# One pending weight subtraction, placed ahead of the closing steps of the output projection

## The chip, the cores and the metric

The kernel runs on one core of one Trainium2 chip. The metric is the device time of one execution in microseconds (us); less is better. The core has a matrix engine (PE, whose weight loads PEld overlap the products), a vector engine (DVE), a scalar engine (ACT), a second elementwise engine (POOL), and a queue engine (SP) that issues nearly all DMAs. Each engine works through its own instructions in program order and waits on semaphores for the others.

## The reference

One decoder layer over x of 512 tokens by 2048 channels, all in float32:

```
h = rms_norm(x);  proj = h @ w_in          # 30 column tiles of 128
out_a, out_b, out_c = dilated attention, convolution module, sliding-window attention
x = x + concat(out_a, out_b, out_c) @ w_out          # output projection, residual
h2 = rms_norm(x)
x = x + (silu(h2 @ w_gate) * (h2 @ w_up)) @ w_down   # D_FF = 5632
```

The change lies between the third line and the first product with w_gate.

## The kernel before, in words

Tokens lie along the free axis (512 columns), channels along the 128 partitions. Weights come from HBM as units of 128 x 1024 float32. To keep float32 precision each unit is split into two fp32r parts: a high part `wh` (a cast on ACT) and a low part `wl = w - wh` (a subtraction on DVE, line 221). Products are then summed from high and low parts.

The units are numbered in the order of their use: 0 to 60 for the input projection, 61 to 92 for the output projection (two passes over the 16 column tiles, one unit for each tile and pass), and from 93 on for the feed-forward part. There the matrices gate, up and down are multiplied in seven products of half size in place of eight (a Strassen form). Each group takes four weight blocks called 11, 12, 21 and 22, and sums of them called s; its seven products use the units s, 11, 21, s, 12, 22, s in this order, with the operands number 5, 1, 7, 6, 2, 4, 3 of the activations. The first group is g0, the first of gate: units 93 (s), 94 (11), 95 (21), 96 (s), 97 (12), 98 (22), 99 (s).

`next_unit()` hands out unit u and emits the split of unit u+2 (`split_up_to`), so a split runs two units ahead. The low part's subtraction is first put into the list `lows`. While the list `late_lows` is filled (from the input projection to the end of the output projection), it stays there until the next call of `lows_now()`, which comes with the next unit; afterwards it is emitted at once. In the second pass of the output projection, from its third tile on, and in all that follows, ACT casts each unit twice (lines 240 and 241): into a PSUM tile `wn`, from which DVE subtracts, and into the SBUF tile `wh`. There are three `wh`, three `wl` and two PSUM buffers.

`Ticks` is an order written out by hand: a step is entered as due so many ticks later, `tick()` emits what is due, and `drain()` emits all that is left. In the second pass a tile has two ticks. The steps on a finished tile n of x2 = x + mix @ w_out are: `residual` (line 825: the PSUM sum into x), a tick later `scale_x2` (the store to DRAM, and the product with the norm's gain on ACT), then `differences` (lines 855 or 861 to 863 on DVE: the operand sums of the Strassen form) and `square_x2` (for the norm), then `high` (ACT, line 869) and `low` (DVE, line 875), which make the operands `h5_j`, `h1_j` and so on for the feed-forward products. The tiles come in the order 0, 8, 1, 9, ..., 7, 15.

After the last tile (n = 15, unit 92) `ticks.drain()` emits what is left: the low parts of the operands of pair 6, the differences of tile 7, `residual` of tile 15, and all that follows from these two tiles. Then line 912 calls `lows_now()`, which emits the subtraction of unit 94, the one still pending, and, where a raw weight buffer is free, further loads (`pump`). Only then does the first group begin: `next_unit()` for unit 93, with the sum s + 11 on DVE (line 176) and the split of unit 95 ahead of it.

A product of the feed-forward part is `Block.multiply`: eight matmuls with the high weights over 512 columns (the operand's high and low half side by side), and eight with the low weights over 256 columns. `flip` alternates the order: unit 93 takes the high weights first and then the low ones, unit 94 the low ones first, unit 95 the high ones first, and so on.

The norm's factor is worked out within the first group: `norm2a` after unit 95 (eight small matmuls, line 303, one DVE step on line 369, a power on POOL, line 370), `norm2b` after unit 96 (four transposes, line 309).

Of the kernel before, what the change touches and what calls it, by code (L numbers as in the profile page):

```python
# [109 lines left out]
def kernel(ctx: ExitStack, tc: tile.TileContext, xT, wi, wo, wgu, wd, cst_in, outT):  # L110
# [8 lines left out]
    def open_banks(**pools):  # L119
        if psum:  # L120
            psum.pop("stack").close()
        psum["stack"] = ctx.enter_context(ExitStack())
        for name, bufs in pools.items():
            psum[name] = psum["stack"].enter_context(
                tc.tile_pool(name=f"{name}{len(pools)}", bufs=bufs, space=bass.MemoryType.PSUM))
# [7 lines left out]
    def bank(name, cols=T):  # L133
        return psum["banks"].tile([P, cols], F32, name=name, tag="b")
# [71 lines left out]
    def pump(limit):  # L206
        while at["entry"] < len(entries) and len(raws) < limit and entries[at["entry"]][0] not in held:
            buf, key, parts = entries[at["entry"]]
            t, o = take(buf, key, sum(p.shape[-1] for p in parts)), 0
            for part in parts:  # L210
                nc.sync.dma_start(t[:, o:o + part.shape[-1]], part)
                o += part.shape[-1]
            at["entry"] += 1
# [4 lines left out]
    def lows_now():  # L218
        while lows:
            fn, *args = lows.pop(0)  # L220
            fn(*args)  # L221
        if late_lows:
            pump(RAW_EARLY if at["use"] <= 20 else RAW_BUFS)
# [28 lines left out]
    def next_unit():  # L252
        sums_now()
        u = at["use"]
        at["use"] += 1
        lows_now()
        split_up_to(u + SPLIT_AHEAD)
        if not lows:
            pump(RAW_EARLY if u < 20 else RAW_BUFS)
        return splits.pop(u)  # L260

    def mm3(out, wh, wl, xh, xl, start, stop):
        nc.tensor.matmul(out, wh, xh, start=start, stop=False)  # L263
        nc.tensor.matmul(out, wh, xl, start=False, stop=False)  # L264
        nc.tensor.matmul(out, wl, xh, start=False, stop=stop)  # L265
# [540 lines left out]
    def load_x(i):  # L806
        if i < KT:
            n = OUT_ORDER[0][i]
            xr[n] = slot(f"xr{n}")
            nc.sync.dma_start(xr[n], xT[n])  # L810
# [66 lines left out]
    def split_rows(k):  # L877
        for name in ROWS[k:k + 3]:
            if name in mix:
                split_mix(name)  # L880
# [4 lines left out]
    for half in range(2):  # L885
        for i, n in enumerate(OUT_ORDER[half]):
            if half == 1 and i == 2:
                ticks.drain()
                b = None
                open_banks(banks=4, high=2)  # L890
            b = bank(f"o{half}_{n}")
            wh, wl = next_unit()
            for kk in range(8):
                k = 8 * half + kk
                row = ROWS[k]
                while row not in m_hi and row not in mix:
                    ticks.tick()
                split_rows(k)
                s = slice(kk * P, (kk + 1) * P)
                mm3(b, wh[:, s], wl[:, s], m_hi[row], m_lo[row], kk == 0, kk == 7)  # L900
                if kk % 4 == 3 or i == 0:
                    ticks.tick()
            ticks.after(0, residual, n, b, half)
            if half == 0:
                load_x(i + 2)
        for row in ROWS[8 * half:8 * half + 8]:
            if half == 0:
                m_hi.pop(row), m_lo.pop(row)
    ticks.drain()
    m_hi = m_lo = r1b = mult_a = bias_a = bias_c = None  # L910

# [323 lines left out]
```

## Time and profile before

| | |
|---|---|
| median of 3 runs | 1929.77 us (1929.02 to 1929.9) |
| the profiled execution, time | 1930.23 us |
| the profiled execution, span of its instructions | 1928.4 us |
| mean granted clock of PE | 0.995 |
| DVE busy | 1470.9 us (76%) |
| ACT busy | 1328.8 us (69%) |
| POOL busy | 985.3 us (51%) |

The span runs from the first to the last instruction of the profiled execution; the time of an execution holds a little besides. A row of the timeline reads: start, length, engine, line of the kernel, operation, output and inputs, shapes, the number of merged instructions, and in brackets how long the engine sat idle before it and what released it. An instruction's length includes what overlaps with the next one, so the distance from start to start is often shorter than the length. A row of the view by stretches gives the stretch, its length, the busy time of each engine with the number of instructions, the granted clock of PE (PEclk, 1.00 is full speed), the busy share of the DMA engines and the GB/s.

### The profile page before, as it was taken

How to read it: one execution, taken by the hardware profiler on the slowest of the kernel's cores; microseconds unless marked ns; L12 is line 12 of the kernel's file. 1: busy time of each engine (PE TensorE's matmuls, PEld its weight loads, DVE VectorE, ACT ScalarE, POOL GpSimd, SP SyncE). 2: the span in 40 equal slices, each digit the busy share in tenths (PEclk: the TensorE clock that was granted, in tenths of full speed). 3: DMA queues.
4: the chain of work that ended last, by engine and by line, in shares of the span. 5: the costliest groups of instructions: out<-in, count | busy, mean ns of one | idle time of the engine just before them, and what ended most of it. 6: DMA issues, size and time to landing. Idle time of an engine off the chain costs nothing.

```text
span 1928.4 us, 29205 instructions
## 1 busy us (share of the span) xinstructions
PE 1897.9 (98%) x10332; PEld 1644.2 (85%) x10332; DVE 1470.9 (76%) x2512; ACT 1328.8 (69%) x1782; POOL 985.3 (51%) x636
## 2 busy tenths in 40 slices
PE   8999999989999999999999999999999999999999
PEld 7888788878887888888888888888888788888888
DVE  6799989997578677777777777777777577767776
ACT  6356555553356788788888888888887577667675
POOL 0111011000000788778887878788776656656564
PEclk9999999999999999999999999999999899999999
DMA  7232222223342344444444444353438978777685
GB/s 264 76 102 70 66 88 77 72 77 115 131 135 73 129 160 162 139 160 167 160 142 156 162 158 155 138 179 139 173 126 302 363 274 278 267 247 272 198 281 194
DMA packets 125651, 319.48 MB, mean 166 GB/s; under 512 B 14016, under 2 KB 29504, under 8 KB 125504
## 3 DMA queue, kind: packets, MB, share of 16 engines
q1 hardware_dynamic: 125360, 317.51, 47.8%
q8 instruction: 81, 1.33, 0.3%
q14 instruction: 66, 0.54, 0.1%
q10 hardware_dynamic: 144, 0.10, 0.0%
HBM read 259.09 MB, written 57.15 MB: 164 GB/s over the span
## 4 chain that ended last, share of the span: by engine, by line
PE 71%; DMA 1%; DVE 0%; issue 0%; ACT 0%; SPq 0%; DVEq 0%
PE out L966 66%; PE o L264 1%; PE o L263 1%; PE o L265 1%; DMA a<-od 1%; DMA od<-u21st 0%; DVE h L875 0%; DVE xr L825 0%; DVE ssum L90 0%; DVE wl L221 0%; ACT wn L240 0%; ACT wh L241 0%; PE n2b L303 0%; DVE ml_b L753 0%; PE r2s L309 0%
## 5 line engine op out<-in xcount | busy, mean ns | idle before, releaser
L966 PE MATMUL out<-h,wh 128*128 128x512 f32 x2464 | 590.4, 392 | 0.1
L966 PEld LDWEIGHTS out<-h,wh 128*128 128x128 f32 x2464 | 454.8, 189 | 88.0 <-DVE h L875 0.6
L966 PEld LDWEIGHTS out<-h,wl 128*128 128x128 f32 x2464 | 316.9, 192 | 15.7 <-DVE wl L221 3.8
L966 PE MATMUL out<-h,wl 128*128 128x256 f32 x2464 | 321.1, 284 | 3.6 <-DVE wl L221 3.6
L966 PE MATMUL out<-a,wh 128*128 128x512 f32 x1232 | 300.3, 395 | 3.0 <-DMA a<-od 2.0
L966 PEld LDWEIGHTS out<-a,wh 128*128 128x128 f32 x1232 | 227.4, 190 | 49.9 <-DMA a<-od 3.6
L234 ACT CAST wh<-w 128x1024 fp32r<-128x1024 f32 (+1 forms) x93 | 96.8, 1041 | 131.4 <-PE o L264 48.2
L966 PEld LDWEIGHTS out<-a,wl 128*128 128x128 f32 x1232 | 160.9, 193 | 10.6 <-DMA a<-od 4.1
L966 PE MATMUL out<-a,wl 128*128 128x256 f32 x1232 | 164.6, 285 | 2.3 <-DMA a<-od 2.3
L221 DVE TENSOR_TENSOR wl<-w,wh 128x1024 fp32r<-128x1024 f32 (+1 forms) x93 | 112.4, 1209 | 30.1 <-ACT wh L234 29.9
L978 DVE TENSOR_TENSOR y<-y,out 128x256 f32<-128x256 f32 x120 | 50.5, 421 | 65.8 <-PE out L966 62.1
L442 DVE SCALAR_TENSOR_TENSOR y<-bu,cst,y 128x511 f32<-128x511 f32 (+14 forms) x120 | 88.7, 739 | 0.5
L370 POOL TENSOR_TENSOR n2r<-n2v,nhalf 128x4 f32<-128x4 f32 x1 | 1.0, 1010 | 162.3 <-DVE n2v L369 162.3
L264 PE MATMUL o<-ml_c,wh 128*128 128x512 f32 x128 | 50.4, 394 | 3.3 <-DVE ml_c L753 3.3
L979 DVE TENSOR_TENSOR y<-y,out 128x256 f32<-128x256 f32 x120 | 50.5, 421 | 4.1
L263 PE MATMUL cq<-hh,wh 128*128 128x512 f32 x128 | 51.3, 401 | 0.0
L263 PE MATMUL o<-mh_c,wh 128*128 128x512 f32 x128 | 51.0, 399 | 0.0
L265 PE MATMUL o<-mh_c,wl 128*128 128x512 f32 x128 | 50.1, 391 | 0.0
L265 PE MATMUL cq<-hh,wl 128*128 128x512 f32 x128 | 50.1, 391 | 0.0
L264 PE MATMUL cq<-hl,wh 128*128 128x512 f32 x128 | 50.0, 391 | 0.0
L825 DVE TENSOR_TENSOR xr<-xr,o 128x512 f32<-128x512 f32 x32 | 21.9, 685 | 21.7 <-PE o L265 21.7
L264 PEld LDWEIGHTS o<-ml_c,wh 128*128 128x128 f32 x128 | 24.1, 188 | 9.2 <-DVE ml_c L753 4.8
(3092 smaller groups left out, 4817.4 us busy)
## 6 DMA issues: line engine op xcount, KB each, us to landing
a<-od SPq DMA_DIRECT2D x196, 256.0 KB, 5.4
w<-in_wi SPq DMA_DIRECT2D x59, 512.0 KB, 3.6
w<-in_wo SPq DMA_DIRECT2D x32, 512.0 KB, 3.6
y<-x2d SPq DMA_DIRECT2D x48, 256.0 KB, 5.5
x2d<-y SPq DMA_DIRECT2D x64, 128.0 KB, 3.4
x<-in_xT SPq DMA_DIRECT2D x16, 256.0 KB, 7.2
xr<-in_xT SPq DMA_DIRECT2D x16, 256.0 KB, 3.9
x2d<-xr SPq DMA_DIRECT2D x16, 256.0 KB, 2.0
```

What stands on the lines that cost most here:

```text
L221: fn(*args)
L234: nc.scalar.copy(hi[:, :n], t[:, :n])
L263: nc.tensor.matmul(out, wh, xh, start=start, stop=False)
L264: nc.tensor.matmul(out, wh, xl, start=False, stop=False)
L265: nc.tensor.matmul(out, wl, xh, start=False, stop=stop)
L370: nc.gpsimd.tensor_tensor(r, v, nhalf[:, :NT], op=ALU.pow)
L442: nc.vector.scalar_tensor_tensor(yconv[j][:, i:], hconv[j][:, :T - i], c, yconv[j][:, i:], op0=ALU.mult, op1=ALU.add)
L825: nc.vector.tensor_add(t, t, b)
L966: nc.tensor.matmul(out, lhs[:, s], rhs, start=begin, stop=x is xs[-1] and low == flip[0], skip_group_check=True)
L978: sign(out, out if first is None else first, main)
L979: sign(out, out, rest)
```

## The change

One line is added behind the two passes of the output projection:

```diff
@@ -906,6 +906,7 @@
         for row in ROWS[8 * half:8 * half + 8]:
             if half == 0:
                 m_hi.pop(row), m_lo.pop(row)
+    lows_now()
     ticks.drain()
     m_hi = m_lo = r1b = mult_a = bias_a = bias_c = None
 
```

`lows_now()` is:

```python
    def lows_now():
        while lows:
            fn, *args = lows.pop(0)
            fn(*args)
        if late_lows:
            pump(RAW_EARLY if at["use"] <= 20 else RAW_BUFS)
```

So the pending subtraction of unit 94 stands on DVE ahead of everything that `ticks.drain()` emits, and the call on line 912 finds the list empty. No instruction is added or removed.

## The prediction

> **What bounds the kernel now.** I read the page's totals first, then the stretches behind the changed place, then the timeline around it.
>
> ```profile
> span 1928.4 us, 29205 instructions
> PE 1897.9 (98%) x10332; PEld 1644.2 (85%) x10332; DVE 1470.9 (76%) x2512; ACT 1328.8 (69%) x1782; POOL 985.3 (51%) x636
> ```
>
> ```profile
> 640.00:1480.00 840.00, 840.00 (x4830) 742.97 (x4829) 627.53 (x861) 690.71 (x819) 671.77 (x431) 1.00 0.45 158
> 1480.00:1516.00 36.00, 30.72 (x130) 22.50 (x129) 17.81 (x29) 17.12 (x25) 14.85 (x13) 0.86 1.05 391
> 1516.00:1928.40 412.40, 408.64 (x2347) 360.90 (x2345) 296.45 (x458) 284.59 (x316) 247.96 (x158) 1.00 0.75 257
> ```
>
> PE sets the end. From 640 to 1480 us it is busy in 840.00 of 840.00 us, so what arrives earlier at 640 arrives earlier at 1480. From 1480 to 1516 the DMA engines are full (1.05) and PE waits for them; behind that PE is busy again in 408.64 of 412.40 us. A microsecond won on PE near 620 therefore counts, unless the stretch at 1480 swallows it.
>
> The timeline at the changed place, all engines, cut to the rows I use:
>
> ```profile
> 608.23 1.00 ACT L240 CAST wn<-w('11', 'g0')_5530 128x1024 fp32r<-128x1024 f32 x1
> ...
> 613.18 0.42 DVE L875 TENSOR_TENSOR h<-ta,h 128x256 fp32r<-128x256 f32 x1
> ...
> 614.86 0.42 DVE L855 TENSOR_TENSOR ta<-h 128x256 f32<-128x256 f32 x1
> ...
> 615.68 0.40 ACT L869 CAST h<-h 128x256 fp32r<-128x256 f32 x1
> ...
> 616.63 0.69 DVE L825 TENSOR_TENSOR xr<-xr,o 128x512 f32<-128x512 f32 x1 [1.35 <-PE o L265]
> ...
> 617.35 0.72 ACT L835 ACTIVATE h<-xr,cst 128x512 f32<-128x512 f32 x1 [1.26 <-DVE xr L825]
> ...
> 618.30 0.19 PEld L966 LDWEIGHTS out<-h,wh 128*128 128x128 f32 x1 [0.55 <-DVE h L875]
> ...
> 618.64 1.12 PE L966 MATMUL out<-h,wl 128*128 128x256 f32 x8
> ...
> 621.65 1.04 ACT L241 CAST wh<-w('21', 'g0')_5427 128x1024 fp32r<-128x1024 f32 x1
> ...
> 622.04 1.22 DVE L221 TENSOR_TENSOR wl<-w('11', 'g0')_5530,wn 128x1024 fp32r<-128x1024 f32 x1
> 623.17 1.22 DVE L176 TENSOR_TENSOR w('s', 'g0')_5630<-w('s', 'g0')_5630,w('11', 'g0')_5530 128x1024 f32<-128x1024 f32 x1
> ...
> 623.31 2.08 PE L966 MATMUL out<-h,wl 128*128 128x256 f32 x8 [3.55 <-DVE wl L221]
> ```
>
> PE ends unit 93 (the rows at 618.30 and 618.64) and then sits idle for 3.55 us until the low part of unit 94, which is multiplied first, is there (622.04 + 1.22 = 623.26). Its input `wn` was cast long before (608.23 + 1.00 = 609.23): the subtraction waited for nothing but its place in DVE's queue, behind the last steps on x2. The idle time has a second price, which the stretches show in the column PEclk:
>
> ```profile
> 618.96:622.38 3.42, 0.80 (x7) 0.59 (x5) 3.39 (x9) 3.31 (x7) 0.00 (x0) 1.00 0.00 0
> 622.38:625.79 3.41, 2.48 (x10) 2.39 (x11) 3.41 (x4) 1.68 (x3) 0.00 (x0) 0.50 0.00 0
> 625.79:629.20 3.41, 3.41 (x10) 2.64 (x9) 2.50 (x3) 1.91 (x3) 0.00 (x0) 0.50 0.75 234
> ```
>
> After a stretch with PE busy for only 0.80 of 3.42 us the granted clock falls to 0.50, and stays there until 629.20. So the units 94 and 95 run at half speed.
>
> **The change part by part.** Nothing is added or removed: one DVE subtraction moves up.
>
> The new place. What `drain` emits on DVE begins with the row at 613.18 (low parts of pair 6), then the differences of tile 7 (614.86), then `residual` of tile 15 (616.63). The subtraction now stands before 613.18. Its `wn` is ready, and the `wl` buffer that it takes is unit 91's, whose products were over when the last tile began, so it should run at once. It holds DVE for 1.13 us (622.04 to 623.17), and the six operations behind it slip by that. The cover is the 1.35 us for which DVE stood idle before 616.63, since `residual` waits for PE's last product. That leaves 0.2 us. On ACT the casts behind the differences slip from 615.68 to 616.81, ending at 617.2, in front of the scaling at 617.35, which waited 1.26 us; it does not move. So the operand for unit 93's last pair comes as before (618.30). Without that cover unit 93 would end up to 1.13 us later, and no more.
>
> SP's and POOL's queues. The call also runs `pump`, now ahead of x2's last stores. It should issue nothing there: the next load, u0's block 21, needs the raw buffer that g0's 21 holds until unit 95 is split. In the trace it goes out right behind that split's subtraction; it will come with it, about 1.1 us earlier. POOL has nothing to do there.
>
> ```profile
> 624.30 1.22 DVE L221 TENSOR_TENSOR wl<-w('21', 'g0')_5427,wn 128x1024 fp32r<-128x1024 f32 x1
> 624.42 1.02 ACT L240 CAST wn<-w('s', 'g0')_5630 128x1024 fp32r<-128x1024 f32 x1 [1.73 <-DVE w('s', 'g0')_5630 L176]
> ...
> 625.48 1.22 DVE L221 TENSOR_TENSOR wl<-w('s', 'g0')_5630,wn 128x1024 fp32r<-128x1024 f32 x1
> 625.59 0.33 SPq L211 DMA_DIRECT2D w('21', 'u0')_5913<-in_wgu  x1
> ...
> 626.79 1.23 DVE L176 TENSOR_TENSOR w('s', 'g0')_5630<-w('s', 'g0')_5630,w('12', 'g0')_5633 128x1024 f32<-128x1024 f32 x1
> ...
> 628.84 0.69 DVE L973 TENSOR_REDUCE g0u<-out 128x256 f32<-128x512 f32 x1 [0.82 <-PE out L966]
> ...
> 629.45 1.21 DVE L221 TENSOR_TENSOR wl<-w('12', 'g0')_5633,wn 128x1024 fp32r<-128x1024 f32 x1
> ...
> 631.69 0.95 PE L303 MATMUL n2b<-ones,ssum 128*128 128x1 f32 x8
> ...
> 632.50 1.20 PE L966 MATMUL out<-h,wl 128*128 128x256 f32 x8
> ...
> 632.67 0.16 DVE L369 TENSOR_SCALAR n2v<-n2b 128x4 f32<-128x4 f32 x1 [2.02 <-PE n2b L303]
> ...
> 632.92 1.01 POOL L370 TENSOR_TENSOR n2r<-n2v,nhalf 128x4 f32<-128x4 f32 x1 [162.34 <-DVE n2v L369]
> ...
> 633.53 2.00 PE L966 MATMUL out<-h,wh 128*128 128x512 f32 x8
> ...
> 635.38 0.60 PE L309 MATMUL r2s<-ident,n2r 128*128 128x128 f32 x4
> ```
>
> Term 1, the idle time. Eight low matmuls take 8 x 0.12 us at full clock (1.12 us less the 0.28 us length of the last, over 7). Unit 94 starts at 618.64 + 0.96 = 619.60 in place of 623.31: 3.71 us won.
>
> Term 2, the clock. From 623.31 to the norm's matmuls at 631.69 the units 94 and 95 took 8.38 us. At full clock a high matmul costs 0.23 us (2.00 less 0.39 over 7), so two units are 16 x 0.23 + 16 x 0.12 = 5.6 us: 2.78 us won.
>
> Term 3, what is late next. Unit 94 would end at 619.60 + 0.96 + 1.84 = 622.40, but unit 95 begins with its high part, which ACT finishes at 622.69 behind its own x2 steps, unmoved. PE starts 0.05 us behind that (as 623.31 behind 623.26) and loses another 0.1 us on a start after a stall (618.30, next product 618.64): 0.44 us lost. Unit 95's low part comes by 623.17 + 1.22 = 624.39 and is needed at 624.7, so it is hidden, by 0.3 us. The norm's matmuls then start at about 625.65.
>
> Term 4, the norm's factor. DVE now does, one behind the other: the sum s + 11 at 622.04, unit 95's subtraction at 623.17, unit 96's at 624.35 (its cast starts at 623.29 and takes 1.02), the sum with 12 at 625.66 (1.31 behind, as now), the reduction at 626.8, unit 97's subtraction at 627.4, the norm's step at 628.55. POOL follows 0.25 us later and takes 1.01: 629.8. The transposes could start on PE at 625.65 + (635.38 - 631.69) = 629.34, and wait until 629.85: 0.51 us lost. DVE's queue takes the stalled place here, but only for half a microsecond.
>
> Sum: 3.71 + 2.78 - 0.44 - 0.51 = 5.54 us. It is the same as the distance of the transposes, 635.38 to 629.85. From there on all starts about 5.5 us earlier. On the profiled execution (1930.23 us, span 1928.4 and 1.8 us around it) that gives 1924.7; the median of the runs lies 0.46 us below that execution, so I predict 1924.3.
>
> A rule weighed against the row. The row says: 0.80 us busy in 3.42 us was enough for the half clock. The Trainium skill, "TensorE: Matmul & The Clock Gate", Part 1, has the clock halved after an idle window of about 3.4 us, in windows that run free of the kernel. A gap of 3.55 us would hold such a window whole in few executions only; by that rule most runs of before had no half clock, and term 2 would be missing (the first rival below gives that time from rows). This trace does not bear the rule out to the letter, as its window was not idle.
>
> **The rivals.**
>
> First, the clock term is not in the timed runs. Then before starts the norm's matmuls at 623.31 + 5.6 = 628.9 and its transposes at 632.6; against 629.85 the gain is 2.75 us and the time 1927.0. For it: the fall of the clock hangs on where the gap lies. Against it: three runs lie within 0.9 us of each other and within 1.2 us of the profiled one that has the term.
>
> Second, the change doesn't do what it says: the subtraction is held by a buffer until PE's last product of the projection, or the stall goes over to another wait of the same length, such as unit 95's high part. The rows speak against it. ACT's cast is unmoved and done at 622.69, so the longest stall that can follow is the 0.44 us above; and held until 616.6 the subtraction costs unit 93 the 1.13 us that I priced. What is left is a wait that no row shows. It would give about 1929.5.
>
> Third, the other side: the stretch from 1480 to 1516, where the clock falls too.
>
> ```profile
> 1496.19:1499.60 3.41, 2.25 (x9) 1.20 (x8) 0.84 (x2) 0.00 (x0) 0.00 (x0) 1.00 1.05 402
> 1499.60:1503.02 3.42, 2.25 (x6) 1.25 (x4) 0.00 (x0) 0.00 (x0) 1.55 (x1) 0.50 1.04 389
> ...
> 1506.43:1509.84 3.41, 3.41 (x15) 3.17 (x15) 0.00 (x0) 0.53 (x1) 3.33 (x5) 0.50 1.04 405
> ```
>
> Here 2.25 of 3.41 us busy were enough, and the half clock held for 10.2 us. All changes of the clock in these rows lie whole multiples of 3.41 us apart (622.38, 629.20, 1499.60, 1509.84), so work that comes 5.5 us earlier is shifted against them by 1.6 such windows, and the clock may fall earlier here, or stay down into the stretch in which PE is full again. A window of full work at half clock costs 1.71 us. From the fourth further window on (6.8 us) it eats the whole gain; with five the time is 1924.3 + 8.5 = 1932.8. Against it: a window with PE busy throughout ended it both times, and while PE waits for DMA a slow clock costs little. It may as well shorten; I allow 1.7 us, one window, either way inside the forecast.
>
> **How the numbers follow.** The forecast (gap and half clock both gone) has 0.78, the first rival 0.10, the second 0.08, the third 0.04. The predicted time is the forecast's, 1924.3. Its own bounds are 1923.3 (the terms 1 and 2 whole, 6.49 us) and 1925.4 (unit 93 late by 1.13), and a window of the clock either way widens them to about 1922.2 and 1926. The upper end is taken to 1927.2, over the first rival's 1927.0; the second and third stay outside. What a measurement of this kernel can tell from no change is about 0.2%, 3.9 us, so faster means below 1925.9. Most of the forecast's 0.78 lies below that, and some of its upper tail above (0.03); of the first rival a fifth lies below. That gives 0.77 faster, 0.19 same; slower 0.04.
>
> **What would show it.** In the profile after, the subtraction for unit 94 stands before the low parts of pair 6, near 613, and the sum s + 11 at about 622.0; `residual` of tile 15 stays at 616.6 and PE's wait for unit 93's last operand at 618.3. PE's 3.55 us before unit 94 are gone, and waits of under 0.6 us stand before unit 95 (for ACT's high part) and before the transposes (for POOL). PEclk is 1.00 from 616 to 640, and the transposes start near 629.85. The prediction is wrong if PE still waits over 1 us between 619 and 631, if the clock falls there all the same, if `residual` comes later than 617, or if a shift of 5.5 us at 640 is no longer there at 1480 or at 1516.

## The result and the profile after

The changed kernel takes 1924.94 us (median of 10 runs, 1924.54 to 1925.71); the kernel before, on the same chip, 1929.72 us (10 runs, 1928.81 to 1930.06). The ratio is 0.9976, with a 95% interval of 0.9968 to 0.9984: 4.78 us less by the medians, where 5.5 were forecast. The profiled execution of the changed kernel took 1925.47 us.

First the page of the changed kernel, then its stretches.

```profile
span 1923.7 us, 29204 instructions
PE 1897.1 (99%) x10332; PEld 1642.1 (85%) x10332; DVE 1470.4 (76%) x2512; ACT 1328.8 (69%) x1782; POOL 986.6 (51%) x636
```

```profile
616.00:624.00 8.00, 7.67 (x40) 6.07 (x39) 7.71 (x19) 5.61 (x12) 0.00 (x0) 1.00 0.09 33
624.00:632.00 8.00, 7.75 (x48) 6.61 (x47) 7.84 (x11) 6.54 (x8) 2.55 (x2) 1.00 0.69 227
640.00:1480.00 840.00, 840.00 (x4832) 742.42 (x4831) 627.94 (x863) 688.64 (x818) 671.67 (x431) 1.00 0.46 160
1516.00:1923.70 407.70, 403.86 (x2320) 356.40 (x2318) 291.93 (x450) 279.82 (x309) 245.79 (x157) 1.00 0.74 256
```

Every engine does the same work as before, and the span is 4.7 us shorter: what went is time in which PE stood or ran slowly. PEclk is 1.00 through the changed place, and PE is busy in 15.4 of 16 us there. The timeline at that place:

```profile
613.88 1.22 DVE L221 TENSOR_TENSOR wl<-w('11', 'g0')_5530,wn 128x1024 fp32r<-128x1024 f32 x1
...
616.68 0.41 DVE L855 TENSOR_TENSOR ta<-h 128x256 f32<-128x256 f32 x1
...
617.12 2.38 PE L967 MATMUL out<-h,wh 128*128 128x512 f32 x8
...
617.32 0.69 DVE L825 TENSOR_TENSOR xr<-xr,o 128x512 f32<-128x512 f32 x1 [0.22 <-PE o L265]
...
619.00 0.19 PEld L967 LDWEIGHTS out<-h,wh 128*128 128x128 f32 x1 [0.55 <-DVE h L875]
...
619.33 2.08 PE L967 MATMUL out<-h,wl 128*128 128x256 f32 x16
...
622.73 1.22 DVE L176 TENSOR_TENSOR w('s', 'g0')_5630<-w('s', 'g0')_5630,w('11', 'g0')_5530 128x1024 f32<-128x1024 f32 x1
623.45 1.68 PEld L967 LDWEIGHTS out<-h,wh 128*128 128x128 f32 x8 [0.62 <-ACT wh L241]
...
626.34 1.02 PE L303 MATMUL n2b<-ones,ssum 128*128 128x1 f32 x8
...
629.22 0.15 DVE L369 TENSOR_SCALAR n2v<-n2b 128x4 f32<-128x4 f32 x1
...
630.51 0.65 PE L309 MATMUL r2s<-ident,n2r 128*128 128x128 f32 x4 [0.25 <-POOL n2r L370]
```

The sixteen low matmuls from 619.33 are unit 93's and unit 94's in one run: nothing stands between them any more. All starts are 0.69 us late in this profile, as unit 93 begins at 617.12 in place of 616.43. Line numbers behind the added line are one higher. So the steps are measured from unit 93's first product:

| from unit 93's first product, us | before | forecast | after |
|---|---|---|---|
| unit 94's first product | 6.88 | 3.17 | 3.17 |
| unit 95's first product | | 6.31 | 6.33 |
| the norm's matmuls | 15.26 | 9.22 | 9.22 |
| the norm's step on DVE | 16.24 | 12.12 | 12.10 |
| the transposes | 18.95 | 13.42 | 13.39 |

(Unit 94's start after is 619.33 plus eight times 0.12, less 617.12.) Within this place the gain is 18.95 - 13.39 = 5.56 us, and 5.54 was forecast. The 0.69 us lie ahead of it, where the code of both kernels is the same. They can be traced to a place: a weight cast on ACT (line 234) is still 0.51 us earlier in the changed kernel's profile (213.35 in place of 213.86), and a later cast of the same line is 0.78 us late (240.83 in place of 240.05). In between the granted clock was halved for two windows of 3.41 us in this profile, and for one in that of the kernel before. First the stretches of the changed kernel, then those of the kernel before:

```profile
224.76:228.17 3.41, 2.87 (x11) 2.58 (x12) 2.90 (x8) 3.30 (x8) 0.00 (x0) 0.50 0.02 6
228.17:231.59 3.42, 3.42 (x13) 2.93 (x12) 3.25 (x13) 0.95 (x3) 0.00 (x0) 0.50 0.53 153
```

```profile
226.43:229.84 3.41, 3.41 (x12) 2.73 (x11) 2.87 (x8) 2.41 (x6) 0.00 (x0) 0.50 0.00 0
229.84:233.26 3.42, 3.42 (x20) 2.93 (x19) 3.28 (x11) 1.76 (x6) 0.00 (x0) 1.00 0.56 158
```

From the one cast to the other it is 27.3 to 27.5 us in the three profiles that have two halved windows here (this one, and e4 and e6 below, which keep the order of before), and 26.0 to 26.2 us in the other six, e7 of the changed kernel among them. So the delay belongs to the execution and not to the change. A half clock later in the attention part did not add to it:

```profile
419.33:422.74 3.41, 1.40 (x7) 0.79 (x6) 3.34 (x9) 3.05 (x5) 0.00 (x0) 1.00 0.77 277
422.74:426.16 3.42, 2.29 (x5) 1.38 (x5) 3.35 (x10) 1.72 (x3) 0.00 (x0) 0.50 0.28 107
426.16:429.57 3.41, 3.02 (x9) 2.46 (x10) 3.36 (x6) 0.91 (x2) 0.00 (x0) 0.50 0.00 0
```

The first profile of before has the full clock there, and yet the changed kernel lies 0.74 us behind it ahead of this place (line 689 on ACT, 410.20 and 409.46) and 0.72 us behind it after (line 716 on ACT, 438.96 and 438.24).

### The profile page after: what moved, and what is told of

It reads as the page before. It is cut to its first block, busy times and chain, and to the rows that moved or that the text cites. A ratio compares the mean times of both kernels' runs of the same rounds, so it can differ in the third digit from the quotient of the medians.

```text
span 1923.7 us, 29204 instructions
## 1 busy us (share of the span) xinstructions
PE 1897.1 (99%) x10332; PEld 1642.1 (85%) x10332; DVE 1470.4 (76%) x2512; ACT 1328.8 (69%) x1782; POOL 986.6 (51%) x636
## 4 chain that ended last, share of the span: by engine, by line
PE 81%; issue 9%; DVE 8%; DMA 1%; ACT 1%; POOL 0%; DVEq 0%; SPq 0%; POOLq 0%; ACTq 0%
PE out L967 66%; DVE y L442 2%; DVE wl L221 1%; PE cq L263 1%; PE cq L265 1%; PE cq L264 1%; DMA a<-od 1%; PE in L263 1%; PE in L264 1%; PE in L265 1%; PE o L264 1%; PE o L265 1%; PE o L263 1%; PE ak L263 0%; PE aq L263 0%
## 5 line engine op out<-in xcount | busy, mean ns | idle before, releaser
L263 PE MATMUL in<-hh,wh 128*128 128x512 f32 x64 | 25.8, 403 | 5.9 <-ACT wh L234 5.9
```

## The experiments

The distance from unit 93's first product to the transposes is used below as the measure of the place, since it is free of what lies ahead.

**The gap filled (e1).** The order of before, with 15 products that serve no purpose in PE's idle time; they are computed in addition, and the output does not use them.

```diff
                 blk.multiply(q, w, [ops[q, j] for j in range(NJ)])
+                if g == 0 and i == 0:
+                    for d in range(15):
+                        s = slice((d % 8) * P, (d % 8 + 1) * P)
+                        nc.tensor.matmul(outs[2], w[0][:, s], ops[q, d % 8], start=True, stop=True,
+                                         skip_group_check=True)
```

> The kernel before, with 15 further products of unit 93's high weights behind unit 93, into a PSUM bank that unit 95 starts anew. Their results are not used. They fill PE's 3.55 us in front of unit 94 but leave its low part where it was, so the idle time is still lost (15 x 0.23 = 3.4 us of filler). My theory (the gap costs twice, as idle time and as half clock): unit 94 still starts near 623.3, but PEclk stays at 1.00 and the norm's matmuls start at 628.9 to 629.4 in place of 631.7; DVE's order then holds the transposes at about 632.6. Gain over the kernel before 2 to 2.8 us, time about 1927.3. Rival (the clock falls for another reason, or half clock costs little here): PEclk still falls near 622, time within 0.7 us of the kernel before.

Measured: 1927.3 us against 1929.44, ratio 0.9988 (0.998 to 0.9997). The timeline of PE, and the stretches of the same kernel:

```profile
615.98 2.38 PE L966 MATMUL out<-h,wh 128*128 128x512 f32 x8
...
619.15 3.59 PE L1137 MATMUL out<-h,wh 128*128 128x512 f32 x15
...
622.85 1.22 PE L966 MATMUL out<-h,wl 128*128 128x256 f32 x8
...
623.91 3.82 PE L966 MATMUL out<-h,wh 128*128 128x512 f32 x16
...
632.20 0.60 PE L309 MATMUL r2s<-ident,n2r 128*128 128x128 f32 x4
```

```profile
620.00:624.00 4.00, 3.89 (x22) 3.08 (x21) 4.00 (x8) 2.28 (x5) 0.00 (x0) 1.00 0.00 0
624.00:628.00 4.00, 4.00 (x21) 3.35 (x20) 3.91 (x4) 3.87 (x4) 0.00 (x0) 1.00 0.43 135
```

Unit 94 starts as late as before (622.85 - 615.98 = 6.87 us) and the clock stays up: the sixteen high products take 3.82 us where they took 5.71, and the transposes come 16.22 us behind unit 93's first product, with 16.2 expected (632.6 less 616.43). PE does 15 products more, and the kernel is 2.14 us faster. So the idle time itself halved the clock, and the half clock has a price of its own. The rival that it costs little falls.

**The subtraction one tick later (e2).**

```diff
+    ticks.tick()
     lows_now()
     ticks.drain()
```

> The changed kernel, with the pending subtraction one tick later: behind the low parts of pair 6, the differences of tile 7 and residual of tile 15, ahead of the low parts of pair 7. My theory (what counts is that DVE's whole queue ends at the same time, and a later end of unit 93 is hidden behind the waits for ACT and POOL): unit 93's last operand comes 1.13 us later (PE waits 1.7 us for DVE line 875 in place of 0.55), the wait of unit 95 for ACT goes, the one of the transposes shrinks to under 0.3; the transposes move by 0.2 us at most and the time is that of the changed kernel, 1924.9 to 1925.3. Rival (the cover of 1.35 us ahead of residual is what makes the change good): all of the 1.13 us comes through, time about 1926.1.

Measured: 1925.46 us, ratio 0.998 (0.9971 to 0.9988); the times alone do not tell it from the changed kernel. The timeline does:

```profile
616.08 0.69 DVE L825 TENSOR_TENSOR xr<-xr,o 128x512 f32<-128x512 f32 x1 [1.35 <-PE o L265]
616.68 1.21 DVE L221 TENSOR_TENSOR wl<-w('11', 'g0')_5530,wn 128x1024 fp32r<-128x1024 f32 x1
...
618.89 0.19 PEld L968 LDWEIGHTS out<-h,wh 128*128 128x128 f32 x1 [1.68 <-DVE h L875]
...
622.62 1.22 DVE L176 TENSOR_TENSOR w('s', 'g0')_5630<-w('s', 'g0')_5630,w('11', 'g0')_5530 128x1024 f32<-128x1024 f32 x1
623.33 1.70 PEld L968 LDWEIGHTS out<-h,wh 128*128 128x128 f32 x8 [0.61 <-ACT wh L241]
...
630.40 0.65 PE L309 MATMUL r2s<-ident,n2r 128*128 128x128 f32 x4 [0.25 <-POOL n2r L370]
```

Unit 93's first product is at 615.88 in this run, so the transposes lie 14.52 us behind it, in place of 13.39: the whole 1.13 us comes through, as the rival said. What I had expected of unit 93 came (1.68 us of waiting), but I took the later waits as fixed in time, and they are not. Behind `residual` the subtraction no longer fills the 1.35 us in which DVE waits for PE, so DVE's queue ends 1.13 us later (line 176 is 6.74 us behind unit 93's first product, as before the change, where the changed kernel has 5.61). ACT's casts for tile 15 wait for DVE's differences, and unit 95's weights are cast behind them, so they move too: unit 95 starts 7.45 us behind unit 93's first product in place of 6.33, and the wait for ACT stays at 0.61 us. The cover is worth its 1.13 us.

**The norm's matmuls one unit earlier (e3),** on top of the changed kernel.

```diff
 def norm2a():
-        b = psum["high"].tile([P, 1024], F32, name="n2b", tag="h")
+        b = outs[3]
...
-            if g == 0 and i in (2, 3):
-                (norm2a if i == 2 else norm2b)()
+            if g == 0 and i in (1, 3):
+                (norm2a if i == 1 else norm2b)()
```

> The changed kernel, with the norm's eight small matmuls behind unit 94 in place of unit 95, and their result in the PSUM bank that unit 96 starts later. My theory (two waits are left, 0.3 to 0.44 us for ACT ahead of unit 95 and 0.5 for POOL ahead of the transposes): the small matmuls run while PE would wait for ACT, the norm's step stands on DVE ahead of unit 97's subtraction, the wait for POOL is gone; the transposes start 0.75 us earlier than in the changed kernel, time about 1924.2. Rival (DVE's and ACT's work up to unit 97 sets the pace whatever the order): the wait moves to unit 96 or 97, with no gain, 1924.9.

Measured: 1923.53 us, ratio 0.9971 (0.9959 to 0.9982), the lowest of all. Its timeline:

```profile
615.48 2.38 PE L967 MATMUL out<-h,wh 128*128 128x512 f32 x8
...
621.46 0.95 PE L303 MATMUL out<-ones,ssum 128*128 128x1 f32 x8
...
622.27 2.11 PE L967 MATMUL out<-h,wh 128*128 128x512 f32 x8
...
624.53 0.15 DVE L369 TENSOR_SCALAR n2v<-out 128x4 f32<-128x4 f32 x1
...
627.96 0.60 PE L309 MATMUL r2s<-ident,n2r 128*128 128x128 f32 x4
```

The small matmuls fill the wait for ACT, and the wait for POOL is gone: 12.48 us to the transposes, 0.91 less than in the changed kernel. So terms 3 and 4 of the forecast were these two waits, and they can be had as well. In the times 0.9976 and 0.9971 lie within each other's intervals; that e3 is faster rests on the trace.

**The loads alone (e4).** Only the second half of the added call stands at the new place.

```diff
+    pump(RAW_BUFS)
     ticks.drain()
```

> The kernel before, with only the second half of the added call at the new place: the weight loads that could be issued, but not the subtraction. My theory: no raw buffer is free there, so nothing moves; 1929.7, PE's idle time ahead of unit 94 stays 3.55 us. Rival (part of the gain came from loads that go out ahead of x2's stores): faster by 0.5 us or more, with a weight load on SP's queue before 625.

Measured: 1929.8 us, ratio 1.0001 (0.9992 to 1.001). The timeline:

```profile
615.84 2.38 PE L967 MATMUL out<-h,wh 128*128 128x512 f32 x8
...
622.72 2.07 PE L967 MATMUL out<-h,wl 128*128 128x256 f32 x8 [3.54 <-DVE wl L221]
624.59 4.50 PE L967 MATMUL out<-h,wh 128*128 128x512 f32 x16
...
624.99 0.33 SPq L211 DMA_DIRECT2D w('21', 'u0')_5913<-in_wgu  x1
...
633.57 0.60 PE L309 MATMUL r2s<-ident,n2r 128*128 128x128 f32 x4
```

The gap stands as before, and the first load behind it goes out at 624.99, behind unit 95's subtraction: 9.15 us behind unit 93's first product, with 9.16 before (625.59 less 616.43). The loads have no part in the gain. But the sixteen high products take 4.50 us here, against 5.71 in the first profile of before, for the same work. That led to the next runs.

**The kernel before, profiled twice more (e5, e6), and the changed kernel on that chip (e7).** No edits.

> The kernel before, unchanged, looked at again. In its first profile the clock is halved for two windows of 3.41 us at the changed place and unit 93's first product and the transposes lie 18.95 us apart (616.43 to 635.38); in the run with the loads alone, whose work is the same, for one window, and 17.73 us apart (615.84 to 633.57). My theory (where the gap lies against windows that run free of the kernel decides): the distance falls between 17.5 and 19.0, with one or two windows of half clock that start within 4 us of the gap's start. Rival (the two lengths come from the kernels, not from chance): 18.9 to 19.0 and two windows in each look at this kernel.

> The same kernel and the same two theories once more: the distance between 17.5 and 19.0 with one or two windows, against 18.9 to 19.0 with two in each look.

> The changed kernel, timed on the chip of these looks. My theory (the gap's idle time of 3.71 us less 0.9 us of new waits, and the half clock, which the filled gap priced at 2.1 us on average): 4.6 to 5.0 us faster than the kernel before; in the profile no half clock between 600 and 640, and 13.4 us from unit 93's first product to the transposes, as in its first profile (617.12 to 630.51). Rival (the half clock costs 2.8 us in every run, as the forecast's term had it): 5.5 us faster.

Measured: the stretches of e5, then those of e6, cut at the changes of the clock and the 3.41 us ahead of them.

```profile
617.79:621.20 3.41, 1.28 (x9) 1.04 (x9) 3.34 (x10) 2.94 (x8) 0.00 (x0) 1.00 0.12 44
621.20:624.61 3.41, 1.99 (x9) 1.99 (x10) 3.41 (x4) 1.68 (x2) 0.00 (x0) 0.50 0.00 0
624.61:628.02 3.41, 3.41 (x10) 2.64 (x10) 2.63 (x3) 2.04 (x3) 0.00 (x0) 0.50 0.59 178
628.02:631.43 3.41, 3.41 (x24) 3.05 (x22) 1.82 (x2) 2.48 (x3) 0.00 (x0) 1.00 0.81 299
```

```profile
620.03:623.44 3.41, 0.09 (x1) 0.09 (x1) 3.41 (x8) 2.71 (x5) 0.00 (x0) 1.00 0.00 0
623.44:626.86 3.42, 3.42 (x12) 3.05 (x13) 3.33 (x4) 2.39 (x3) 0.00 (x0) 0.50 0.01 5
626.86:630.27 3.41, 3.41 (x19) 2.90 (x18) 2.95 (x3) 1.99 (x3) 0.00 (x0) 1.00 0.91 334
```

In e5 the clock is down for two windows, and the transposes come 18.73 us behind unit 93's first product (615.74 to 634.47); in e6 for one window, and 17.79 us (616.47 to 634.26). The same kernel gives both. The fall lies 5.46 us behind unit 93's first product in e5 (621.20 less 615.74) and 6.97 in e6 (623.44 less 616.47), so the windows do not start with the kernel's work. Where the clock fell while PE still stood (e5), the first halved window held 1.99 us of work and a second followed; where it fell just when PE started (e6), that window held 3.42 us and was the only one. The first profile of before (2.48 us, then a second window) and e4 (3.35 us, the only one) go the same way. That the work in the first window decides is an inference from these four, and other places do not bear it out as a rule: in the stretch around 1500 a halved window with 2.73 us was the last (the changed kernel, from 1494.52), and one with 3.13 us was not (before, from 1503.02).

e7 has 13.40 us to the transposes (615.44 to 628.84), as the first profile of the changed kernel. Its time is 1924.15 us against 1929.62, ratio 0.9974 (0.9964 to 0.9984): 5.5 us by the medians and 5.0 by the ratio, so the time alone does not decide between my 4.6 to 5.0 and the rival's 5.5. The four profiles with the gap do: the clock's price is not the same in each run.

## Why the prediction held, and where it was off

- The mechanism held in each step: the subtraction waited for its place alone, the six steps behind it on DVE were covered (`residual` waits 0.22 us for PE after, 1.35 before, and 0.2 was forecast), unit 93's end did not move, and SP's loads kept their place behind unit 95's subtraction (the first at 625.14 after, that subtraction from 623.87 for 1.21 us). The prediction named `residual` later than 617 as a sign of being wrong, and it comes at 617.32. That is the 0.69 us from far ahead: it stands 0.20 us behind unit 93's first product in both profiles (616.63 less 616.43, 617.32 less 617.12).
- Term 1, the idle time, was 3.71 us as forecast.
- Terms 3 and 4, the waits that come in its place: unit 95's start is 0.02 us from the forecast and the transposes 0.03. e3 takes both waits away and wins 0.91 us, with 0.95 forecast for the two.
- Term 2, the clock, is the one mis-sized for an average execution. I took 2.78 us from one, in which the clock was down for two windows. The four profiles with the gap (before, e4, e5, e6) have 18.95, 17.73, 18.73 and 17.79 us to the transposes, and e1, with the gap filled, 16.22: the half clock cost 2.73, 1.51, 2.51 and 1.57 us, 2.08 on average, and by e1's time 2.14. With 2.1 in place of 2.78 the sum is 4.9 us. The timings cannot choose between the two sums: they gave 4.78 and 5.47 us by the medians, and the interval of the first runs from 3.1 to 6.2 us. For the profile that it was read from the term was right (2.73), so that 5.56 meets 5.54 within the place tests the other terms, and not what the clock costs in other executions. That the spans of the first two profiles differ by 4.7 us, about as the medians do, is luck: 5.56 us won at the place, 0.69 lost far ahead of it.
- Two details of the prediction do not come out of its own rows. The units 94 and 95 did not run at half speed to their end: the clock was back at 629.20, ahead of unit 95's low products (630.73, eight in 1.12 us as at full clock). Term 2 is not touched by it, being taken from start to start. And the lower bound of 1922.2 follows from none of the terms: the forecast with one window of 1.7 us either way gives 1922.6 and 1926.0, and the forecast's own bounds, widened by as much, 1921.6 and 1927.1. The measured 1924.94 us lies inside all of them.
- The first rival (no clock term in the timed runs) falls by e1, and its gain of 2.75 us lies just outside the interval of 3.1 to 6.2 us. Its time of 1927.0 lies inside the predicted range, so a hit in that range alone would not have told it from the forecast. The rival's reason was half right: the windows run free of the kernel, but all four profiles with the gap have the fall, and what varies is its length. The rule of the Trainium skill ("TensorE: Matmul & The Clock Gate", Part 1), an idle window of about 3.4 us, was met to the letter in e4 (PE busy for 0.00 us from 619.24 to 622.66) and nearly so in e6 (0.09 us); in e5 a window with 1.28 us of work was enough. The length of 3.41 us agrees.
- The second rival falls by the timeline after: the longest new wait of the weight loads is 0.68 us, and 0.25 for the products.
- The third rival did not come. Between 1480 and 1516 the clock was down for 6.8 us after the change and 10.2 before; it was 6.8 us in e4, e5 and e6 too, with the order of before, so this difference is not the change's. The stretch let the gain through: PE's wait for ACT behind it ended at 1507.85 in place of 1512.64, 4.79 us earlier. The rows of the kernel before and of the changed kernel:

```profile
1512.64 1.88 PE L966 MATMUL out<-a,wh 128*128 128x512 f32 x7 [0.96 <-ACT wh L241]
```

```profile
1507.85 1.89 PE L967 MATMUL out<-a,wh 128*128 128x512 f32 x7 [1.08 <-ACT wh L241]
```

From the transposes to the end of the span it is 1293.0 us before (1928.4 less 635.38) and 1293.2 after (1923.7 less 630.51), and 1292.8 to 1293.8 in all nine profiles. What is won at the place reaches the end, to within that scatter of 1 us.

## What to carry to other kernels

Where an engine that sets the end waits for another, look at what the awaited instruction itself waited for: if its inputs were ready long before, it is only its place in a queue, and a place just ahead of that queue's own idle time costs nothing as long as it is shorter than that idle time (1.13 of 1.35 us here). Price a PE gap with the slow products behind it, and take that price from several executions, since one shows only one position of the clock's windows. When two orders are compared, add up the queue to its end: an operation that no longer fills an idle time moves everything behind it, on the engines that wait for it too.

## What the hardware showed unexpectedly

- The clock fell after a 3.41 us window with 1.28 us of PE work (e5), 1.40 (the changed kernel at 419) or 2.25 (before at 1496), so a window need not be idle. But it did not fall after one with 1.63 us (before, from 417.57, sixty windows ahead of the fall at 622.38), so PE's busy time, as the profile gives it, does not decide by itself. What else does stays open.
- It came back after windows with 3.41 and 3.42 us of work (e5, e6), and not after one with 1.99 (e5). Between these there is no clear line: 2.73 us was enough in the changed kernel at 1494.52, and 3.13 was not in the kernel before at 1503.02.
- A half clock does not cost the same everywhere: two halved windows in place of one went with 1.1 to 1.5 us more between 214 and 240, and two in place of none with nothing between 410 and 438.
- Fifteen products without use made the kernel 2.14 us faster (e1), by keeping the clock up.
